# The second MLP matrix over the latents by seven block products for eight, with its operands formed where the first matrix leaves

## The chip, the cores and the metric

The kernel runs on one core of a Trainium2 chip. The metric is the device time of one execution in microseconds (us). The core's engines run side by side and meet only at semaphores: PE (TensorE) multiplies matrices, DVE (VectorE), ACT (ScalarE) and POOL (GpSimd) work element by element, and SP (SyncE) issues the transfers between the chip's memory (HBM) and the core's own memory (SBUF). PE leaves its sums in PSUM, in banks of 128 x 512 numbers. Each engine takes its instructions in the order in which the built program lists them, so one that waits holds back all that stand behind it.

## The reference, cut to what matters

Two layers work on 1024 latent tokens and 256 context tokens of width 1024. In each layer three token mixers (attention, a Fourier mix, a gated long convolution) are put together by an output projection, and a squared-ReLU MLP of hidden width 4096 follows. Each sub-layer is normalised and modulated: the six modulation vectors of a layer (shift, scale and gate of either sub-layer) are products of SiLU(c) with `w_mod`.

```
sh1, sc1, g1, sh2, sc2, g2 = modulation(c, w_mod[l], b_mod[l])      # likewise for c_ctx
hx = modulate(rms_norm(x, norm1_g[l]), sh1, sc1)
px = hx @ w_in[l]
...
x = x + g1 * heads_out(att_x, px, hy, w_out[l])
h = modulate(rms_norm(x, norm2_g[l]), sh2, sc2)
x = x + g2 * (square(relu(h @ w_mlp1[l])) @ w_mlp2[l])
if not last:                       # layer 0 alone does the same for the 256 context tokens
    ...
return rms_norm(x, final_norm_g)
```

The change concerns `square(relu(h @ w_mlp1)) @ w_mlp2`, a product of (1024 x 4096) with (4096 x 1024) in each layer, and the modulation vectors of layer 1.

## The kernel before, in words

Everything is kept transposed: channels lie on the 128 partitions, tokens on the free axis. Every fp32 product is made of three fp32r products (`mm3`, L146 to L150): each operand is split into a high part (ACT casts it) and a low part (the operand less its high part), and hi x hi, hi x lo and lo x hi are added up in one PSUM bank. `wsplit` (L138 to L145) splits a weight tile of 128 x 1024, the low part on POOL (L144); `split_sb` (L156 to L158) splits an activation tile, the low part on DVE or, where it is given `G`, on POOL (L158).

The stages of a layer follow each other: normalisation and input projection, attention with the other mixers beside it, the output projection (two calls of `half_k`, over the two halves of the 1024 inputs), the MLP's first matrix (`up`), its second (`down`), and the next layer's normalisation or the final one.

`up` already uses the Winograd form of Strassen's scheme: weights and activations are cut into 2 x 2 blocks, sums and differences of blocks are formed, and seven block products (`prod`) stand for eight. For each of its 16 steps it forms four 128 x 512 blocks of the hidden activations, takes ReLU (L1254) and the square (L1248) on ACT, and stores them in `d_u` in HBM.

`down` is a plain product. For each of eight slices of 512 hidden channels, `load` fetches four tiles of `d_u` and splits them, with the low parts on POOL; `half_k` then runs over four weight tiles (`mg`), three column chunks of tokens (0 to 512, 512 to 1024, and in layer 0 the context, 1024 to 1280) and two halves, 12 matmuls to a PSUM bank. `resid` (L1127, DVE) takes each bank, multiplies it by the gate and adds it to the residual stream `xT` (latents) or `xC` (context). The last slice is done chunk by chunk in `last_passes`, so that the next normalisation can begin behind the first chunk.

The modulation vectors are made on DVE, one instruction with an accumulated output (L171) for each 128 channels and stream; each reads a weight tile `wm` of 512 KB, for which there are two buffers. For layer 1 all six vectors (64 such instructions over 48 tiles) are made as a side job, `late`, under layer 0's `down`.

The side jobs are Python generators: `spawn(rate, job)` adds one to the background and `tick()`, called after each group of matmuls, takes as many steps of it as the rate says. What the order of the instructions on each engine is in the end, a scheduler decides when the program is built; the rows of the built program show it.

## Time and profile before

| | us |
|---|---|
| median of 3 runs (3231.13 to 3231.99) | 3231.6 |
| the profiled execution's own time | 3233.92 |
| its span, first to last instruction | 3232.2 |
| PE busy in the span | 3028.6 (94%) |
| DVE / POOL / ACT busy | 1884.2 / 1514.3 / 1364.2 |

The stages that the change touches, by the profiled execution's own clock (us from the start of the span):

| stage | layer 0 | layer 1 |
|---|---|---|
| output projections | 769 to 895 | 2407 to 2498 |
| first MLP matrix, `up` | 895 to 1322 | 2498 to 2841 |
| second MLP matrix, `down` | 1322 to 1798 | 2841 to 3220 |

A share of busy time is a mean over unlike stages; a stage's own windows say more. Durations are those of one execution, whose own time lies 2.3 us above the median.

### The profile page before, as it was taken

What the parts mean: (1) busy time and instruction counts of PE and PEld (TensorE: products, weight loads), DVE (VectorE), ACT (ScalarE), POOL (GpSimd) and SP (SyncE); (2) the same over time, 40 slices, a digit from 0 to 9 for tenths busy, and PEclk for the clock granted to TensorE, in tenths of its full rate; (3) what the DMA queues carried; (4) which work ended last, traced back from release to release, by engine and by line L of the source; (5) the groups of instructions that cost most, each with busy time, mean ns of one, the idle gap of its engine ahead of it and who ended that gap; (6) DMA issues with size and microseconds to landing.
All of it is one profiled execution on the core that took longest, in us unless ns stands there. A gap on an engine that the chain in (4) does not pass through costs nothing. (4 is left out here: it accounts for less than half of the span.)

```text
span 3232.2 us, 42677 instructions
## 1 busy us (share of the span) xinstructions
PE 3028.6 (94%) x15756; PEld 2516.0 (78%) x15756; DVE 1884.2 (58%) x2909; ACT 1364.2 (42%) x2425; POOL 1514.3 (47%) x987
## 2 busy tenths in 40 slices
PE   5999998999989999999999999998999799999998
PEld 1787886887768888787888787887887688878886
DVE  7895679886485222297324635779874753322226
ACT  4324475675344444321122423576763444432113
POOL 6434437542555444564442324437535655464333
PEclk8999998999999999999999998999999899999998
DMA  6453563434424322657213233743343343362213
GB/s 241 154 194 114 199 182 89 112 96 165 129 98 141 106 97 90 233 199 259 103 68 104 88 110 102 239 124 89 77 176 111 127 157 105 108 228 92 90 60 111
DMA packets 168280, 433.34 MB, mean 134 GB/s; under 512 B 38086, under 2 KB 55911, under 8 KB 167816
## 3 DMA queue, kind: packets, MB, share of 16 engines
q1 hardware_dynamic: 155064, 388.86, 36.9%
q0 software_dynamic: 9504, 34.67, 3.5%
q10 hardware_dynamic: 3504, 7.08, 0.6%
q8 instruction: 125, 2.05, 0.3%
q14 instruction: 83, 0.68, 0.1%
HBM read 326.21 MB, written 104.33 MB: 133 GB/s over the span
## 5 line engine op out<-in xcount | busy, mean ns | idle before, releaser
L144 POOL TENSOR_TENSOR wl<-wr,wh 128x1024 fp32r<-128x1024 f32 (+2 forms) x274 | 650.0, 2375 | 990.7 <-ACT wh L143 985.5
L143 ACT CAST wh<-wr 128x1024 fp32r<-128x1024 f32 (+2 forms) x274 | 277.8, 1014 | 846.7 <-PE pso L149 385.0
L1127 DVE SCALAR_TENSOR_TENSOR xT<-pso,modc,xT 128x512 f32<-128x512 f32 (+1 forms) x328 | 239.5, 735 | 468.3 <-PE pso L150 436.4
L148 PE MATMUL pso<-uh,wh 128*128 128x512 f32 (+1 forms) x1312 | 488.5, 374 | 13.5 <-DVE xT L1127 5.2
L149 PE MATMUL pso<-ul,wh 128*128 128x512 f32 (+1 forms) x1312 | 484.1, 369 | 6.7 <-POOL ul L158 6.6
L150 PE MATMUL pso<-uh,wl 128*128 128x512 f32 (+1 forms) x1312 | 483.6, 369 | 4.1 <-POOL wl L144 4.1
L1027 POOL TENSOR_SCALAR p<-p,st 128x1280 f32<-128x1280 f32 (+1 forms) x144 | 182.9, 1271 | 263.9 <-DVE st L1022 111.9
L148 PEld LDWEIGHTS pso<-uh,wh 128*128 128x128 f32 x1312 | 250.5, 191 | 59.7 <-DVE xT L1127 7.5
L149 PEld LDWEIGHTS pso<-ul,wh 128*128 128x128 f32 x1312 | 251.2, 191 | 53.4 <-POOL ul L158 10.7
L150 PEld LDWEIGHTS pso<-uh,wl 128*128 128x128 f32 x1312 | 250.3, 191 | 49.3 <-POOL wl L144 5.0
L158 POOL TENSOR_TENSOR ul<-ur,uh 128x512 fp32r<-128x512 f32 (+1 forms) x152 | 197.4, 1328 | 66.3 <-ACT uh L157 61.4
L154 DVE TENSOR_TENSOR pt<-pst,pt 128x512 fp32r<-128x512 f32 x328 | 214.7, 681 | 12.0 <-ACT pt L153 10.6
L153 ACT CAST pt<-pst 128x512 fp32r<-128x512 f32 x328 | 181.9, 590 | 85.1 <-PE pst L1048 66.8
L171 DVE SCALAR_TENSOR_TENSOR junk<-wm,crow 128x1024 bf16<-128x1024 f32 x128 | 193.4, 1533 | 38.3 <-DMA wm<-wmod 37.5
L149 PE MATMUL psi<-hl,wh 128*128 128x512 f32 (+1 forms) x536 | 199.4, 372 | 4.9 <-POOL hl L251 2.5
L148 PE MATMUL psi<-hh,wh 128*128 128x512 f32 (+1 forms) x536 | 201.7, 377 | 1.8 <-ACT hh L254 1.1
L150 PE MATMUL psi<-hh,wl 128*128 128x512 f32 (+1 forms) x536 | 198.2, 370 | 3.0 <-POOL wl L144 3.0
L1066 PE MATMUL pv<-pt,v 128*128 128x256 f32 x656 | 172.1, 297 | 15.2 <-DVE pt L154 13.9
L1302 DVE TENSOR_TENSOR wr<-wr 128x512 f32<-128x512 f32 x32 | 37.5, 1173 | 247.7 <-POOL wl L144 242.4
L1067 PE MATMUL pv<-pt,v 128*128 128x256 f32 x656 | 168.0, 292 | 6.0 <-DVE pt L154 5.8
L1048 PE MATMUL pst<-ident,p 128*128 128x128 f32 x1024 | 147.6, 278 | 23.1 <-DVE pt L154 10.9
L1014 DVE TENSOR_REDUCE st<-sx 128x1 f32<-128x1024 f32 x128 | 155.7, 1216 | 14.9 <-PE sx L150 14.3
(413 smaller groups left out, 7580.0 us busy)
## 6 DMA issues: line engine op xcount, KB each, us to landing
wr<-w SPq DMA_DIRECT2D x158, 512.0 KB, 3.6
wm<-wmod SPq DMA_DIRECT2D x80, 512.0 KB, 3.6
d_u<-c SPq DMA_DIRECT2D x128, 256.0 KB, 3.0
ur<-d_u SPq DMA_DIRECT2D x30, 640.0 KB, 5.6
tb<-ftab POOLq DMA_DIRECT2D x34, 512.0 KB, 4.7
ur<-d_u SPq DMA_DIRECT2D x30, 512.0 KB, 4.1
wr<-wout SPq DMA_DIRECT2D x28, 512.0 KB, 4.0
wr<-win SPq DMA_DIRECT2D x26, 512.0 KB, 3.2
```

The costliest lines, as they stand in the source:

```text
L143: S.copy(hi[:, n0:n], t[:, n0:n])
L144: G.tensor_tensor(lo[:, n0:n], t[:, n0:n], hi[:, n0:n].bitcast(F32), op=ALU.subtract)
L148: T.matmul(ps, lhsT=lh, rhs=rh, start=first, stop=False)
L149: T.matmul(ps, lhsT=lh, rhs=rl, start=False, stop=False)
L150: T.matmul(ps, lhsT=ll, rhs=rh, start=False, stop=last)
L153: S.copy(hi, ps)
L154: V.tensor_tensor(lo, ps, hi.bitcast(F32), op=ALU.subtract)
L158: (eng or V).tensor_tensor(lo, src, hi.bitcast(F32), op=ALU.subtract)
L171: V.scalar_tensor_tensor(jk, w, 1.0, crow[:, st, :], op0=ALU.mult, op1=ALU.mult, accum_out=modc[:, l, st, n : n + 1])
L1027: G.tensor_scalar(pr, pr, st[:, 5:6], 1.0, op0=ALU.mult, op1=ALU.mult)
L1066: T.matmul(pv[:, :256], lhsT=vt[:, kt, :], rhs=th, start=j == 0, stop=False)
L1127: V.scalar_tensor_tensor(x, ps[:, : c1 - c0], g, x, op0=ALU.mult, op1=ALU.add)
```

## The change

**Seven products.** In `down`, the first seven of eight parts of the hidden axis (512 channels each, two blocks of 128 pairs: `g` is 0 to 6) are multiplied by the same Winograd form as in `up`. A step (`g`, `j`) takes a weight tile, cut into four blocks of 128 x 256, and makes seven products of six matmuls each (two 128-deep blocks, three fp32r products), where the plain form needs eight. `direct` splits the weight blocks that are used as they are, `combined` forms the four weight combinations on DVE and splits them. Three of the seven products go to the residual at once through `resid`; the other four belong to more than one output block and are added up over all `g` in sums on the core (`sums`; one of them lies in the unused half of `xT`), which `combine` puts together at the end (16 gated additions to `xT` and 16 additions among sums in each layer). The eighth part (`g` 7) is done as before, by `half_k`. The context, in layer 0, keeps its plain product (`context`).

**Operands.** The activations come in seven forms: b11, b21, b22 as they are and t1 to t4, differences of blocks. `up` forms t1 and t3 on DVE and t2 and t4 on POOL for its first 14 steps (`operands`, L1272 to L1281 of the new file), in tiles that it had at hand, and stores seven tiles of 128 x 512 for each step in `d_t` in place of four in `d_u`. `down` fetches and splits them (`fetch`): low parts of t3 and t4, in layer 0 also of t2 and of the context's tiles, on DVE; the others on POOL.

**Modulation.** Layer 1's six vectors are no longer made under layer 0's `down`. Those of its first sub-layer (40 instructions, 24 tiles) are made under layer 0's output projections, those of its second (24 instructions, 24 tiles) under layer 1's.

**Smaller edits.** `last_passes` puts the sums together ahead of the last products of each chunk, and the context's normalisation for layer 1 is begun after the others. The two tiles of `d_u` that `up` loaded early for `down` are gone.

```diff
+            def operands(j, b11, b12, b21, b22):
+                t1, t2, t4 = spare
+                V.tensor_tensor(t1, b12, b11, op=ALU.subtract)
+                G.tensor_tensor(t2, b22, t1, op=ALU.subtract)
+                V.tensor_tensor(b12, b22, b12, op=ALU.subtract)
+                G.tensor_tensor(t4, b21, t2, op=ALU.subtract)
+                for name, t in (("t1", t1), ("t3", b12), ("t2", t2), ("t4", t4)):
+                    nc.sync.dma_start(out=d_t[j, name], in_=t)
...
+            pairs = {name: 4 if not ctx and name in ("b11", "t1", "t2") else 3 for name in SEVEN}
+            sums = {n: [ps_.tile([128, 512], F32, name=f"s{n}{j}") for j in range(4)] for n in (1, 6, 7)}
+            sums[5] = [xT[2 * j + 1][0][:, 512:] for j in range(4)]
...
+            def fetch(src, n, pool, tag, bufs, eng):
+                hi, lo = (pool.tile([128, n], F32R, tag=tag, bufs=bufs, name=tag) for _ in range(2))
+                nc.sync.dma_start(out=lo.bitcast(F32), in_=src)
+                split_sb(hi, lo, lo.bitcast(F32), eng)
+                return hi, lo
...
+            def direct(w):
+                a22 = w[:, 768:1024]
+                hi, lo = wsplit(w, 1024 if ctx else 512)
+                if not ctx:
+                    S.copy(hi[:, 768:], a22)
+                    G.tensor_tensor(lo[:, 768:], a22, hi[:, 768:].bitcast(F32), op=ALU.subtract)
+                return hi, lo
+
+            def combined(w):
+                a11, a12, a21, a22 = (w[:, 256 * i : 256 * i + 256] for i in range(4))
+                r = [nt("r") for _ in range(2)]
+                V.tensor_tensor(r[0][:, :256], a21, a22, op=ALU.add)
+                V.tensor_tensor(r[0][:, 256:], r[0][:, :256], a11, op=ALU.subtract)
+                V.tensor_tensor(r[1][:, :256], a12, r[0][:, 256:], op=ALU.subtract)
+                V.tensor_tensor(r[1][:, 256:], a11, a21, op=ALU.subtract)
+                hi, lo = wsplit(r[0], 512)
+                S.copy(hi[:, 512:], r[1])
+                G.tensor_tensor(lo[:, 512:], r[1], hi[:, 512:].bitcast(F32), op=ALU.subtract)
+                return hi, lo
+
+            def product(g, j, n, w, c, name):
+                ps = psp.tile([128, 512], F32, tag="ps", name="psw")
+                for q in range(2):
+                    ks = slice(c + q * 128, c + q * 128 + 128)
+                    mm3(ps, w[0][:, ks], w[1][:, ks], *at[g, name, q], q == 0, q == 1)
+                if n in sums:
+                    t = sums[n][j]
+                    if g == 0:
+                        S.copy(t, ps)
+                    else:
+                        V.tensor_tensor(t, t, ps, op=ALU.add)
+                else:
+                    u, t = {2: (0, 0), 3: (0, 512), 4: (1, 0)}[n]
+                    resid(l, 5, 2 * j + u, t, t + 512, ps, xT)
...
+                later = spawn(2 if last else 1.2, modulation(1, crow, (4, 3, 5) if last else (1, 0, 2), lambda s: (0, 1) if s < 2 else (0,),
+                                                             mod_load))
                 half_k(l, 2, a["wout"][l, 1], cat, chs, xT, psp, raw[4])
-                finish()
+                settle(jobs)
...
             for (c0, c1), ac, g in todo:
+                if c0 == 512:
+                    settle(later)
```

In the built program the matmuls of 128 x 512 on the MLPs' second matrix fall from 2976 to 2640 over both layers; those of 128 x 256, the context's and the last half chunk's, stay at 960.

Three places show how the order moves. Line numbers shift: L1127 becomes L1136 (`resid`), L144 L153 (`wsplit`), L158 L167 (`split_sb`), L171 L180 (modulation).

The first is DVE in layer 0's output projections, in the second group of weight columns, before (`pso` is a finished bank, `cat` a split tile of the mixers' outputs):

```order
L1127 SCALAR_TENSOR_TENSOR xC_7426<-pso,modc,xC_7426 128x256
L158 TENSOR_TENSOR cat_10241_7960<-wr,cat_10240_7959 128x256
L1127 SCALAR_TENSOR_TENSOR xC_7428<-pso,modc,xC_7428 128x256
L1127 SCALAR_TENSOR_TENSOR xT_7429<-pso,modc,xT_7429 128x512
L1127 SCALAR_TENSOR_TENSOR xT_7431<-pso,modc,xT_7431 128x512
L1127 SCALAR_TENSOR_TENSOR xT_7429<-pso,modc,xT_7429 128x512
L1127 SCALAR_TENSOR_TENSOR xT_7431<-pso,modc,xT_7431 128x512
```

The same place in the change, where `junk,modc<-wm,crow` is a modulation instruction:

```order
L180 SCALAR_TENSOR_TENSOR junk,modc<-wm,crow 128x1024
L1136 SCALAR_TENSOR_TENSOR xT_7529<-pso,modc,xT_7529 128x512
L180 SCALAR_TENSOR_TENSOR junk,modc<-wm,crow 128x1024
L1136 SCALAR_TENSOR_TENSOR xC_7528<-pso,modc,xC_7528 128x256
L1136 SCALAR_TENSOR_TENSOR xC_7530<-pso,modc,xC_7530 128x256
L167 TENSOR_TENSOR cat_01_8054<-wr,cat_00_8053 128x512
L167 TENSOR_TENSOR cat_5121_8056<-wr,cat_5120_8055 128x512
L167 TENSOR_TENSOR cat_10241_8058<-wr,cat_10240_8057 128x256
L180 SCALAR_TENSOR_TENSOR junk,modc<-wm,crow 128x1024 x4
L1136 SCALAR_TENSOR_TENSOR xT_7531<-pso,modc,xT_7531 128x512
```

Modulation instructions, one to four at a time, now stand between the instructions that empty PE's banks.

The second place is layer 1's `down`, away from its ends. DVE before did nothing there but empty banks:

```order
L1127 SCALAR_TENSOR_TENSOR xT_25597<-pso,modc,xT_25597 128x512
L1127 SCALAR_TENSOR_TENSOR xT_25598<-pso,modc,xT_25598 128x512
L1127 SCALAR_TENSOR_TENSOR xT_25591<-pso,modc,xT_25591 128x512
L1127 SCALAR_TENSOR_TENSOR xT_25592<-pso,modc,xT_25592 128x512
L1127 SCALAR_TENSOR_TENSOR xT_25591<-pso,modc,xT_25591 128x512
```

DVE in the change, about one step (`psw` is a finished bank, `s` a sum, `r` a combination of weight blocks, `t_...` an operand's low part):

```order
L1136 SCALAR_TENSOR_TENSOR xT_26559<-psw,modc,xT_26559 128x512
L1421 TENSOR_TENSOR xT_26559<-xT_26559,psw 128x512
L1402 TENSOR_TENSOR r<-wr 128x256
L1405 TENSOR_TENSOR r<-wr 128x256
L167 TENSOR_TENSOR t_28736<-t_28736,t_28735 128x512
L1421 TENSOR_TENSOR s_26582<-s_26582,psw 128x512
L1403 TENSOR_TENSOR r<-r,wr 128x256
L1136 SCALAR_TENSOR_TENSOR xT_26558<-psw,modc,xT_26558 128x512
L1404 TENSOR_TENSOR r<-wr,r 128x256
L1421 TENSOR_TENSOR s_26586<-s_26586,psw 128x512
L1421 TENSOR_TENSOR s_26579<-s_26579,psw 128x512
```

DVE now has seven banks to empty in a step, four weight combinations and a low part or two among them.

The third place is SP's queue where layer 0's `down` begins. Before, the first splits' sources came behind the last stores of `up` but for two (`ur` is a tile of `d_u`):

```order
L1249 DMA d_u_134<-c 128x256
L134 DMA wr<-w 128x1024 x2
L1339 DMA ur<-d_u_103 128x256
L1339 DMA ur<-d_u_104 128x256
L1339 DMA ur<-d_u_105 128x1280
L134 DMA wr<-w 128x1024
L1339 DMA ur<-d_u_106 128x1280
L1249 DMA d_u_134<-c 128x512 x2
```

In the change:

```order
L1365 DMA t_12787<-d_t0t_137 128x512
L1365 DMA t_12792<-d_t0t_140 128x512
L1365 DMA t_12807<-d_t0t_141 128x512
L1258 DMA d_u_134<-c 128x256
L1365 DMA t_12822<-d_t1t_144 128x512
L1365 DMA t_12827<-d_t1t_147 128x512
L1365 DMA t_12842<-d_t1t_148 128x512
L1365 DMA t_12993<-d_t2t_151 128x512
L1365 DMA t_13106<-d_t2t_154 128x512
L143 DMA wr<-w 128x1024
L1365 DMA t_13153<-d_t2t_155 128x512
L1365 DMA b_12797<-d_t0b_135 128x512
```

The operands t2, t3 and t4 of the first products, whose tiles lie where `up` needs nothing any more, are now fetched ahead of all others.

## Rows read from the trace of the kernel before

**Rows 1.** The page: busy time by engine; the chain that ended last.
```profile
PE 3028.6 (94%) x15756; PEld 2516.0 (78%) x15756; DVE 1884.2 (58%) x2909; ACT 1364.2 (42%) x2425; POOL 1514.3 (47%) x987
...
PE 23%; DVE 4%; POOL 1%; ACT 1%; issue 1%; DMA 1%; ACTq 0%; POOLq 0%; DVEq 0%
```

**Rows 2.** Windows of the stages: length, busy time by engine, granted clock, DMA share, GB/s.
```profile
1322.00:1798.00 476.00, 459.07 (x2322) 385.81 (x2322) 267.32 (x364) 112.79 (x171) 223.57 (x136) 0.99 0.46 164
...
2498.00:2841.00 343.00, 323.37 (x1355) 258.41 (x1354) 168.17 (x199) 152.29 (x231) 187.00 (x96) 0.97 0.38 122
2841.00:3220.00 379.00, 366.72 (x1652) 301.18 (x1652) 132.15 (x176) 93.37 (x135) 174.59 (x103) 0.98 0.34 115
```

**Rows 3.** Windows: a stretch of layer 1's second matrix, 128x512 matmuls alone.
```profile
2950.00:3180.00 230.00, 230.00 (x998) 187.18 (x997) 68.17 (x88) 47.45 (x61) 94.27 (x55) 1.00 0.23 76
```

**Rows 4.** Timeline, PE: context matmuls, the 1st and 25th (start, us, instruction).
```profile
782.13 0.28 PE L148 MATMUL pso<-cat,wh 128*128 128x256 f32 x1
...
784.95 0.40 PE L148 MATMUL pso<-cat,wh 128*128 128x512 f32 x1
```

**Rows 5.** Windows: layer 0's second matrix while the modulation runs beside it.
```profile
1380.00:1540.00 160.00, 150.94 (x761) 126.56 (x760) 136.80 (x191) 27.89 (x43) 86.28 (x46) 0.98 0.68 242
1430.00:1480.00 50.00, 46.47 (x226) 39.47 (x226) 43.54 (x57) 9.47 (x15) 30.27 (x16) 0.93 0.61 210
```

**Rows 6.** Groups, 1380 to 1540: count | busy us, mean ns | idle before, who ended it.
```profile
L148 PE MATMUL pso<-uh,wh 128*128 128x512 f32 x166 | 66.9, 403 | 4.9 <-DVE xC L1127 3.8 <-DVE xT L1127 1.1
...
L158 POOL TENSOR_TENSOR ul<-ur,uh 128x512 fp32r<-128x512 f32 x23 | 43.4, 1914 | 31.0 <-ACT uh L157 31.0
...
L148 PE MATMUL pso<-uh,wh 128*128 128x256 f32 x88 | 25.8, 293 | 4.1 <-DVE xT L1127 4.0
```

**Rows 7.** Groups of the page: the modulation instruction, its whole count.
```profile
L171 DVE SCALAR_TENSOR_TENSOR junk<-wm,crow 128x1024 bf16<-128x1024 f32 x128 | 193.4, 1533 | 38.3 <-DMA wm<-wmod 37.5
```

**Rows 8.** Windows: output projections up to the first latent chunk's end, either layer.
```profile
769.00:870.00 101.00, 98.53 (x510) 82.94 (x510) 53.76 (x84) 36.64 (x63) 41.74 (x25) 0.98 0.41 126
...
2407.00:2476.00 69.00, 68.25 (x296) 55.53 (x297) 27.97 (x42) 21.91 (x33) 25.23 (x14) 1.00 0.33 105
```

**Rows 9.** Timeline, DVE near the end (start, us, instruction, idle before it).
```profile
3191.09 0.42 DVE L211 TENSOR_TENSOR facc<-facc,sq 128x256 f32<-128x256 f32 x1 [0.55 <-ACT sq L209]
...
3192.40 2.34 DVE L211 TENSOR_TENSOR facc<-facc,sq 128x256 f32<-128x256 f32 x1 [0.49 <-ACT sq L209]
```

**Rows 10.** Timeline, POOL at the same place.
```profile
3192.08 2.38 POOL L144 TENSOR_TENSOR wl<-wr,wh 128x1024 fp32r<-128x1024 f32 x1 [2.21 <-ACT wh L143]
```

**Rows 11.** Groups, 1560 to 1770, layer 0's second matrix without the modulation.
```profile
L1127 DVE SCALAR_TENSOR_TENSOR xT<-pso,modc,xT 128x512 f32<-128x512 f32 x62 | 46.5, 750 | 109.5 <-PE pso L150 109.5
L144 POOL TENSOR_TENSOR wl<-wr,wh 128x1024 fp32r<-128x1024 f32 x19 | 45.7, 2403 | 120.0 <-ACT wh L143 120.0
...
L158 POOL TENSOR_TENSOR ul<-ur,uh 128x512 fp32r<-128x512 f32 x22 | 28.1, 1296 | 5.7 <-ACT uh L157 5.7
...
L1127 DVE SCALAR_TENSOR_TENSOR xC<-pso,modc,xC 128x256 f32<-128x256 f32 x26 | 12.6, 484 | 20.7 <-PE pso L150 20.7
...
L158 POOL TENSOR_TENSOR ul<-ur,uh 128x256 fp32r<-128x256 f32 x12 | 8.6, 739 | 3.6 <-PE pso L150 3.6
```

**Rows 12.** Groups, DVE, 769 to 832: splits with both sources in SBUF.
```profile
L158 DVE TENSOR_TENSOR cat<-raw,cat 128x512 fp32r<-128x512 f32 x8 | 5.2, 687 | 0.2 <-ACT cat L157 0.2
L158 DVE TENSOR_TENSOR cat<-raw,cat 128x256 fp32r<-128x256 f32 x4 | 1.7, 421 | 0.0
```

**Rows 13.** Groups, DVE, 2600 to 2800, first matrix: SBUF sources; a PSUM source.
```profile
L1303 DVE TENSOR_TENSOR wr<-wr 128x512 f32<-128x512 f32 x12 | 12.6, 1046 | 0.1
...
L1316 DVE TENSOR_TENSOR s<-s,psm 128x512 f32<-128x512 f32 x12 | 8.2, 686 | 27.4 <-PE psm L150 27.4
```

**Rows 14.** Windows: the first 18 and 25 us of the second matrix.
```profile
1322.00:1340.00 18.00, 13.93 (x50) 9.23 (x50) 3.86 (x6) 9.18 (x20) 14.85 (x14) 0.91 0.78 277
2841.00:2866.00 25.00, 18.58 (x70) 13.86 (x70) 6.48 (x10) 12.61 (x22) 19.12 (x14) 0.86 0.69 254
```

More of the change, by code (lines that the diff above doesn't have):

```diff
@@ new lines, in down @@
+            todo = [(g, j) for g in range(7) for j in range(4)]
+            raw = lambda g, j: wload(a["w2"][l, g, j], 1024)
+            parts_of["at"] = 2
+            w = raw(0, 0)
+            C, D = combined(w), direct(w)
+            drain(load(0))
+            load_back()
+            column = {1: (0, "b11"), 2: (256, "b21"), 4: (768, "t4"), 5: (0, "t1"), 6: (256, "t2"), 3: (512, "b22"), 7: (768, "t3")}
+            for n, (g, j) in enumerate(todo):
+                if j == 0:
+                    ahead = spawn(1, load(g + 1))
+                w = raw(*todo[n + 1]) if n + 1 < len(todo) else None
+                order = [6, 7, 1, 5, 4, 2, "D", 3] if n == 0 else [1, 2, 4, "D", 5, 6, 3, 7]
+                if ctx:
+                    order[6:6] = ["c0", "c1", "C"]
+                    if j:
+                        order.remove("D")
+                        order.remove("c0"), order.remove("c1"), order.remove("C")
+                        order[3:3] = ["c0", "c1", "D", "C"]
+                else:
+                    order.insert(order.index("D") + 1, "C")
+                later = C, D
+                for i, what in enumerate(order):
+                    if what == "D":
+                        later = later[0], direct(w) if w is not None else None
+                    elif what == "C":
+                        later = combined(w) if w is not None else None, later[1]
+                    elif what in ("c0", "c1"):
+                        context(g, j, D, int(what[1]))
+                    else:
+                        if j == 3 and what == 5:
+                            settle(ahead)
+                        product(g, j, what, D if what in (1, 2, 4) else C, *column[what])
+                    if i % 3 == 2:
+                        tick()
+                C, D = later
```

285 lines of the change are left out of this document (165 added, 120 removed).

## The prediction

> **What bounds the kernel now.** I read the page first, then windows over the stages, then groups and timelines inside the stages that change. On the page PE is busy for 94% of the span, and the chain that ended last goes mostly through PE [rows 1]: the kernel as a whole is bound by its matmuls. By stages it is the same: layer 0's second matrix takes 476 us with PE busy for 459, layer 1's takes 379 with 367 [rows 2]. A busy PE is a pipelined one, so what a matmul costs is read from its pace. In a stretch of layer 1 without a gap, 998 matmuls of 128x512 take 230.0 us, 0.2305 us each at a granted clock of 1.00, the upper of the two levels (2.4 GHz) [rows 3]; 24 of the context's 128x256 take 784.95 - 782.13 = 2.82 us, 0.1175 each [rows 4]. DVE and POOL have room before: in layer 1's second matrix 132 and 175 us of 379 [rows 2]. The question is what is left of that room when PE has an eighth less to do and they have more.
>
> **The change part by part**, against the profiled execution's own 3233.9 us.
>
> *Matmuls taken away.* The instruction lists give 2976 - 2640 = 336 fewer matmuls of 128x512, 168 a layer: 336 x 0.2305 = **-77.4 us**, all on the path as long as PE is what the stage waits for.
>
> *Modulation out of layer 0's second matrix.* Between 1380 and 1540 DVE is busy for 137 of 160 us, and PE's idle time before new banks, 4.9 + 4.1 us, is ended by DVE's `resid` [rows 5, 6]. In 1430 to 1480 the granted clock is 0.93: 0.07 x 50 = 3.5 us more [rows 5]. With the side job gone I count all of it: **-12.5 us** (from 0, if the new work puts DVE in the same state, a cost that I count below).
>
> *Modulation under the output projections.* One instruction is 1.53 us [rows 7], with the read of its accumulator 1.61. Layer 0 gets 40: 64.5 us. Until its first latent chunk ends, from which the next normalisation starts, DVE has 101 - 53.8 = 47.2 us free [rows 8]; 17 us are left over. In the built order they stand in front of the instructions that empty PE's banks, and the wait is for the chunk's last bank, so DVE's delay passes on to the normalisation and to the first matrix. I take **+17** (0, if PE's eight banks of head start swallow it, to 64, if no idle time can be used). Layer 1 gets 24, 38.7 us, into 69 - 28 = 41 us free [rows 8]; it fits, but the first must wait for its vector to be loaded: **+4** (0 to 39).
>
> *What DVE and POOL do to each other.* Two low parts that read only SBUF show it. A 128x256 addition takes 0.42 us at 3191.09, while POOL is idle, and 2.34 us from 3192.40 to 3194.74; POOL's weight split runs from 3192.08 to 3194.46 [rows 9, 10]. DVE waited for POOL's whole instruction and then did its own 0.3 us later. In the other direction POOL's 128x512 split takes 1.30 us without the modulation beside it and 1.91 with it [rows 6, 11]. Instructions of DVE whose one source is PSUM do not show it: `resid` is 0.75 us [rows 11], an addition from a bank 0.69 [rows 13]. The Trainium skill ("SBUF — State Buffer", Who interferes with whom) states it as a rule: a DVE instruction with two SBUF inputs and a GpSimd one that reads SBUF exclude each other for a whole instruction; the trace agrees, with 2.34 us for 0.42. By that rule POOL's time and DVE's two-source time in a step add up and may not exceed the step, which speaks against this change in layer 1, where it would charge 16 us; without the rule that charge would be nothing.
>
> *A step of layer 1* (one of 28): PE 42 x 0.2305 = 9.68 us. POOL, at the prices of rows 11: two halves of `combined` at 1.30, `direct` 1.30 + 0.74, and 10 operand splits in 4 steps, 2.5 x 1.30: 7.87 us. DVE from PSUM: 3 x 0.75 + 4 x 0.69 = 4.99; from SBUF: four combinations of 256 at 0.42 and one split at 0.69 [rows 12], 2.37. POOL and DVE's SBUF work together are 10.24 us, above PE's 9.68. DVE's waits: in the first matrix its 128x512 combination is 1.05 us instead of 0.69, 0.36 longer [rows 12, 13], with POOL busy for 187 of 343 us, 55% [rows 2]. At 7.87 / 9.68 = 81% that is 0.53, so DVE has 7.36 + 5 x 0.53 = 10.0. I take 10.4 us for a step, a little above both, since queues that are full never line up: 0.72 x 28 = **+20** (0, if the waits fall into gaps, to 117, if each of the five waits for a whole split of 1.30: 13.9 us a step).
>
> *A step of layer 0*: PE 9.68 + 24 x 0.1175 = 12.50 us. POOL 2 x 1.30 + 2.40 + 2 x 1.30 = 7.6; DVE 5.96 from PSUM (two context banks of 0.48 with it) and 3.13 from SBUF, with waits of 0.36 x 0.61 / 0.55 = 0.40 on 6.5 instructions 11.7. Both stay under PE: **+5** for disorder (0 to 27, the 8% that PE lost in rows 5, over 28 steps).
>
> *Putting the sums together.* 32 DVE instructions a layer at about 0.72 us, 23 us, most of them in the last four steps, where layer 1's DVE then has 27 + 23 = 50 us for PE's 39. PE can be eight banks ahead, 8 x 1.38 = 11 us. **+8** for both layers (0 to 20).
>
> *First matrix.* Two more DVE and two more POOL instructions in each of 14 steps a layer, and three more stores. PE hides them: in layer 1 POOL is busy for 55% and DVE for 49% of the stage [rows 2]; in the built order the next weight splits stand ahead of the two that wait for the squares. If that cover failed, 2.6 us of POOL in 28 steps would come out, 73; I take **+2**, as the row on POOL's share is the nearest.
>
> *Start of the second matrix.* PE idles for 4.1 and 6.4 us there and loses 0.09 x 18 and 0.14 x 25 us to the clock, 15 in all [rows 14]. t2, t3 and t4 are now fetched while the first matrix ends, so the first twelve matmuls find their operands; the next ones wait for tiles that come free with the last matmul. **-4** (-15 to +10).
>
> *Transfers.* A step of layer 1 moves 14 tiles of 256 KB over four steps and one of 512 KB, about 148 GB/s where 277 were reached [rows 14]: nothing.
>
> Sum: -77.4 - 12.5 + 17 + 4 + 20 + 5 + 8 + 2 - 4 = **-37.9 us**. The profiled execution lies 2.3 us above the median of 3231.6; on the median this gives 3193.7, say **3194 us**.
>
> **Rivals.** *PE stays the only bound.* The waits of DVE and POOL fall into PE's lead, and nothing is charged for steps and sums: -37.9 - 33 = -70.9, **3161 us**. For it: the first matrix runs a Winograd step with PE busy throughout and DVE's waits hidden. Against it: there POOL was at 55%, here it would be at 81%, and both together above 100%.
>
> *DVE and POOL become the bound in layer 1.* The mechanism is the exclusion shown above, the place layer 1's 28 steps, with layer 0's at 8%: the price 117 - 20 and 27 - 5 more, -37.9 + 119 = +81, **3313 us**. It decides from the point where a step of layer 1 takes 10.4 + 37.9 / 28 = 11.75 us, which is a mean wait of 0.9 us at each of DVE's five SBUF instructions; below that the kernel is still faster. For it: four of the five stand close together, so that each can find the next split of POOL before it, and at 3192.40 the wait was whole. Against it: a DVE that falls behind also feeds POOL later, which then stands less in its way.
>
> *The modulation costs more where it went than it did where it was.* The clock halves in the longer gap before the first matrix, and layer 1's does not fit: 17 + 4 becomes about 45, and the sum -14, **3218 us**. Against it: 24 us of that have no row behind them.
>
> **How the numbers follow.** The forecast has 0.52 (its own range 3172 to 3213), PE alone 0.25, the modulation 0.12, DVE and POOL as the bound 0.11. Leaving out half of the last and the far end of the second, the range is 3150 to 3236. Within 0.2%, 6.5 us, which is about what a measurement of this kernel can tell from no change, I put 0.06, from between the modulation's case and the bound's; faster 0.82, slower 0.12.
>
> **What would show it.** Right: 128x512 matmuls of the second matrix at 0.23 us in the mean of a step in layer 0, and idle time before them in layer 1 that is ended by DVE's additions from banks or POOL's splits, some 20 us; DVE's 256-wide combinations at 0.8 to 1.0 us instead of 0.42; a first matrix of layer 0 that starts 15 us later against the start of the output projections. Wrong: layer 1's second matrix without such gaps and some 310 to 340 us long (PE alone), or longer than its 379 us of before (the bound).

## The result, and the profile after

The changed kernel takes 3285.9 us (median of 4 runs, 3278.97 to 3292.92) against 3231.56: **1.0168 times as long, interval 1.0144 to 1.0192**. Forecast were 3194 us and a range of 3150 to 3236; the sign is wrong. The profiled execution took 3292.92 us, 59.0 more than the one of before; it lies 7.0 us above its median, the one of before 2.3.

The page after, busy time and the chain that ended last, against [rows 1]:

```profile
PE 3002.3 (91%) x15420; PEld 2476.8 (75%) x15420; DVE 2344.2 (71%) x3491; ACT 1480.5 (45%) x2682; POOL 1763.0 (54%) x1165
...
PE 10%; POOL 3%; issue 3%; DVE 2%; DMA 1%; ACT 1%; SPq 0%; POOLq 0%; DVEq 0%; ACTq 0%
```

PE issued the 336 matmuls less, but is busy for only 26 us less in a span that is 59 us longer. The windows of the stages, in order of time, beside [rows 2]: layer 0's output projections and second matrix, layer 1's output projections, first and second matrix (columns as in [rows 2]: length, then busy us of PE, weight loads, DVE, ACT and POOL; clock, DMA share, GB/s).

```profile
776.00:922.00 146.00, 125.21 (x592) 103.11 (x593) 129.36 (x187) 50.55 (x81) 70.38 (x34) 0.91 0.61 204
1353.00:1818.00 465.00, 428.73 (x2152) 360.15 (x2151) 377.04 (x494) 163.14 (x272) 263.98 (x158) 0.96 0.39 132
2432.00:2539.00 107.00, 96.13 (x393) 76.56 (x392) 83.55 (x109) 35.37 (x50) 47.99 (x23) 0.92 0.70 240
2539.00:2892.00 353.00, 326.98 (x1356) 259.11 (x1355) 190.37 (x236) 153.54 (x236) 233.89 (x128) 0.96 0.46 156
2892.00:3279.00 387.00, 346.81 (x1482) 274.10 (x1482) 319.09 (x409) 149.32 (x272) 273.12 (x198) 0.94 0.41 142
```

Layer 1's second matrix was to lose 38.7 us of matmuls and takes 387 us where it took 379. In both second matrices DVE is now busy for more than 80% (it was 56% and 35%), and the granted clock is below 0.97. What PE waited for in the seven-product steps, first layer 0 (1353 to 1748), then layer 1 (2892 to 3211); columns: waited for, us in total, times, longest. `t` and `b` are operands' tiles, `uc` the context's, `wh` and `wl` the weights' high and low parts:

```profile
PE psw L158 <- DVE t L167: 18.7, 6, 5.5
...
PE psw L158 <- POOL b L167: 8.5, 5, 2.9
PE psw L157 <- ACT t L166: 3.8, 1, 3.8
PE psw L159 <- POOL wl L153: 3.3, 1, 3.3
```

In layer 0 there are six waits for an operand's low part in seven groups of four steps: one at each change of group, 8 to 12 us into the new group. In layer 1 the waits end in more places, most often at a low part that POOL itself made. Windows of layer 0 inside a group (four steps' time) and over the next change:

```profile
1430.00:1480.00 50.00, 50.00 (x261) 42.83 (x261) 39.19 (x56) 17.28 (x29) 26.26 (x17) 0.98 0.35 116
1480.00:1535.00 55.00, 52.01 (x261) 44.43 (x260) 44.57 (x62) 16.27 (x27) 31.01 (x21) 0.94 0.33 113
```

Both hold 261 matmuls. Inside a group PE runs without a gap, 12.5 us a step as computed; with a change the same work takes 5 us more, 3 of waiting and about 2 of clock (0.98 - 0.94 = 0.04 of 55 us). The change itself, in three timelines (start, us, instruction, in brackets the idle time before it). PE:

```profile
1480.08 0.40 PE L157 MATMUL psw<-t,wh 128*128 128x512 f32 x1
1483.47 0.79 PE L158 MATMUL psw<-t,wh 128*128 128x512 f32 x1 [2.99 <-DVE t L167]
```

DVE, which makes that low part at 1482.33:

```profile
1473.11 1.52 DVE L1402 TENSOR_TENSOR r<-wr 128x256 f32<-128x256 f32 x1
1474.55 1.52 DVE L1405 TENSOR_TENSOR r<-wr 128x256 f32<-128x256 f32 x1
...
1477.43 1.78 DVE L167 TENSOR_TENSOR t<-t,t 128x512 fp32r<-128x512 f32 x1
1479.14 2.60 DVE L167 TENSOR_TENSOR uc<-uc 128x256 fp32r<-128x256 f32 x1
1481.66 0.74 DVE L1136 SCALAR_TENSOR_TENSOR xT<-psw,modc,xT 128x512 f32<-128x512 f32 x1
1482.33 1.09 DVE L167 TENSOR_TENSOR t<-t,t 128x512 fp32r<-128x512 f32 x1
```

POOL beside it:

```profile
1474.31 2.92 POOL L167 TENSOR_TENSOR b<-b,b 128x512 fp32r<-128x512 f32 x2
1477.19 1.49 POOL L167 TENSOR_TENSOR t<-t,t 128x512 fp32r<-128x512 f32 x1
1478.62 2.83 POOL L153 TENSOR_TENSOR wl<-wr,wh 128x1024 fp32r<-128x1024 f32 x1
1481.42 1.45 POOL L167 TENSOR_TENSOR b<-b,b 128x512 fp32r<-128x512 f32 x1
```

POOL has one split behind the other and no pause. DVE's 256-wide instructions take 1.52, 1.52 and 2.60 us where 0.42 is their own time [rows 12], and the last of them ends 0.3 us after POOL's weight split. Each held the other up: that split takes 2.83 us where 2.40 is its own time [rows 11]. `resid`, which reads a PSUM bank, keeps its 0.74. Over these instructions DVE loses (1.52 - 0.42) x 2 + 1.78 - 0.69 + 2.60 - 0.42 + 1.09 - 0.69 = 5.9 us; PE waits 3.0.

The 59.0 us by stage, from first to last matmul in the two profiled executions. "Main" is the stretch from the first matrix's end to the last passes; in layer 0 its loss is what remains after the matmuls and the modulation are taken off. A group is priced at PE's pace, 4 x 12.50 = 50.0 us in layer 0 and 4 x 9.68 = 38.7 in layer 1:

| | forecast, us | measured, us |
|---|---|---|
| matmuls taken away | -77.4 | -77.4 |
| modulation out of layer 0's second matrix | -12.5 | -14.9 (by the run with the move alone) |
| output projections, layer 0 / layer 1 | +17 / +4 | +20.0 / +16.9 |
| first matrix, layer 0 / layer 1 | +2 in all | +3.0 / +9.4 |
| main of the second matrix, layer 0 / layer 1 | +5 +20 -4 = +21 in all | +38 / +38 = +76 |
| of it, groups 1 to 6, layer 0 / layer 1 | +5 / +20 (all groups) | +31 / +25 |
| of it, group 0 with the stage's start, layer 0 / layer 1 | -4 in all | +6 / +13 |
| last passes, layer 0 / layer 1 | +8 in all | +5.4 / +8.8 |
| stretches that the change doesn't touch, tail | 0 | +7.4 + 3.7 + 0.3 |

Nothing in the change explains the last row; the two executions' distances from their medians differ by 4.7 us.

### The profile page after: what moved, and what is told of

Read it like the earlier page. It is cut to its first block, busy times and chain, and to the rows that moved or that the text cites. A ratio compares the mean times of both kernels' runs of the same rounds, so it can differ in the third digit from the quotient of the medians.

```text
span 3291.1 us, 43722 instructions
## 1 busy us (share of the span) xinstructions
PE 3002.3 (91%) x15420; PEld 2476.8 (75%) x15420; DVE 2344.2 (71%) x3491; ACT 1480.5 (45%) x2682; POOL 1763.0 (54%) x1165
## 5 line engine op out<-in xcount | busy, mean ns | idle before, releaser
L153 POOL TENSOR_TENSOR wl<-wr,wh 128x1024 fp32r<-128x1024 f32 (+2 forms) x274 | 631.2, 2308 | 609.1 <-ACT wh L152 598.0
L152 ACT CAST wh<-wr 128x1024 fp32r<-128x1024 f32 (+2 forms) x274 | 264.8, 968 | 586.4 <-PE psm L158 275.3
L180 DVE SCALAR_TENSOR_TENSOR junk<-wm,crow 128x1024 bf16<-128x1024 f32 x128 | 189.6, 1504 | 35.3 <-DMA wm<-wmod 33.9
L158 PE MATMUL psi<-hl,wh 128*128 128x512 f32 (+1 forms) x536 | 201.1, 375 | 3.8 <-POOL hl L260 2.3
L158 PE MATMUL psw<-t,wh 128*128 128x512 f32 x448 | 181.4, 405 | 23.1 <-DVE t L167 21.5
L157 PE MATMUL psw<-t,wh 128*128 128x512 f32 x448 | 180.4, 403 | 9.9 <-ACT t L166 7.9
L159 PE MATMUL psw<-t,wl 128*128 128x512 f32 x448 | 179.0, 400 | 0.0
L1023 DVE TENSOR_REDUCE st<-sx 128x1 f32<-128x1024 f32 x128 | 155.5, 1214 | 16.0 <-PE sx L159 15.5
L167 POOL TENSOR_TENSOR b<-b,b 128x512 fp32r<-128x512 f32 x96 | 134.7, 1413 | 53.8 <-ACT b L166 48.6
L1029 ACT ACTIVATE p<-sx,st,acol 128x1024 f32<-128x1024 f32 x128 | 153.8, 1201 | 0.0
L1075 PEld LDWEIGHTS pv<-pt,v 128*128 128x128 f32 x656 | 129.5, 197 | 27.5 <-DVE pt L163 20.7
L1136 DVE SCALAR_TENSOR_TENSOR xT<-psw,modc,xT 128x512 f32<-128x512 f32 x168 | 122.6, 741 | 36.3 <-PE psw L159 36.2
L1057 PEld LDWEIGHTS pst<-ident,p 128*128 128x128 f32 x1024 | 118.3, 144 | 37.8 <-issue 16.5
```

What stands on the lines that cost most here:

```text
L152: S.copy(hi[:, n0:n], t[:, n0:n])
L153: G.tensor_tensor(lo[:, n0:n], t[:, n0:n], hi[:, n0:n].bitcast(F32), op=ALU.subtract)
L157: T.matmul(ps, lhsT=lh, rhs=rh, start=first, stop=False)
L158: T.matmul(ps, lhsT=lh, rhs=rl, start=False, stop=False)
L159: T.matmul(ps, lhsT=ll, rhs=rh, start=False, stop=last)
L180: V.scalar_tensor_tensor(jk, w, 1.0, crow[:, st % crow.shape[1], :], op0=ALU.mult, op1=ALU.mult, accum_out=modc[:, l, st, n : n + 1])
```

## The experiments

Theories: **A, handover**: operands come late since their tiles come free late. **B, load**, later sharpened to **D, exclusion**: POOL's splits hold DVE up at the group changes. **C**: the moved modulation. Ratios are to the kernel before, measured anew beside each run (medians 3232 to 3237 us), with 95% intervals; the changed kernel has 1.0168. "Us less" is the difference of two ratios, times 3231.6. Stages are read from each run's profiled execution. The edits are cut to what matters.

**Operands that stay.**
```
-  at[g, name, q] = fetch(...)
+  t = fetch(..., tag of its own); at[g, name, q] = t if g == 0 else at[0, name, q]
```


> The changed kernel, but in the second matrix every product reads the operands of group 0, which stay where they are; those of groups 1 to 7 are fetched and split at the same places as before into a pair of tiles of their own that no matmul reads. So all the work of DMA, ACT, DVE and POOL stays, and no matmul waits for a handed-over operand (the sums over groups 1 to 7 are of the wrong operands). Theory A (handover: at each of the six group changes a layer the next group's operands come late, 55 us a group instead of 50 in layer 0, 43.2 instead of 38.7 in layer 1): 6 x 5 + 6 x 4.5 = 57 us go, 3229 us. Theory B (load: DVE and POOL have too much to do in a step whatever waits for it): the load is the same, 3286 us within 8. Theory C (the moved modulation is what was lost): 3286 too.

1.0295 [1.0272, 1.0319], 3327 us: slower than either theory said. Nothing held the fetches back any more, and the scheduler put the splits of all groups into the first four. Windows of layer 0, with these splits and behind them:

```profile
1420.00:1590.00 170.00, 135.17 (x619) 104.36 (x618) 143.27 (x172) 78.34 (x140) 120.81 (x78) 0.95 0.53 170
1590.00:1740.00 150.00, 149.58 (x788) 127.72 (x789) 106.41 (x165) 26.37 (x36) 59.44 (x36) 1.00 0.14 46
```

So the run doesn't keep the load in its place and can't part A from B. It shows that a loss of this size needs no handover (PE waited there for banks that DVE had not emptied, 15.0 and 13.6 us between 1400 and 1600), and that without operand splits the same steps run at PE's pace.

**Thin splits, both engines; POOL's alone; DVE's alone.**
```
   S.copy(hi, raw)
-  eng.tensor_tensor(lo, raw, hi, op=subtract)
+  eng.tensor_tensor(lo[:, :p], raw[:, :p], hi[:, :p], op=subtract)   # p = 64 from group 1 on
```


> The changed kernel, but the low parts of the second matrix's operands of groups 1 to 7 are formed for 64 of 512 columns only (the other columns keep the unsplit value): order, waits and transfers stay, and about 1.1 us of POOL or 0.6 of DVE goes from each of the 56 (layer 1) or 60 and more (layer 0) operand splits after the first group. Theory A as pure latency (tile free, transfer, copy, split in a row take longer than the 8 us between an operand's last use and its next first use): group changes stay as they are, 3286 - 10. Theory A as a burst in the queues (the refill's splits stand in one row on POOL and DVE): the 57 us of the group changes go for the most part, 3225 to 3245. Theory B (load in all steps): 57 us and more go, 3229 or less, and gaps inside steps go as well as those at the group changes.

> The changed kernel with thin operand splits (64 of 512 columns, other columns unsplit) for POOL's operands alone (b11, b21, b22, t1; in layer 1 t2 too); DVE's stay whole. With both engines' thin, 72 us went. Exclusion (DVE's instructions on SBUF wait for POOL's whole instructions, so that POOL's row at a group's change makes DVE late): 50 to 70 of the 72 go, 3215 to 3236 us, and layer 0's gaps, which DVE's t ends, go too. POOL's own work alone: only layer 1's gaps, which POOL's b ends, go, 3250. DVE's own work: 3270.

> The changed kernel with thin operand splits for DVE's operands alone (t3, t4, in layer 0 t2 and the context's); POOL's stay whole. Exclusion: a thin instruction of DVE still waits for POOL's whole one, and only its own 0.6 us goes: 10 to 25 us, 3261 to 3276. DVE's own work as the cause: layer 0's gaps go, 36 us or more, 3250 or less.

Both 0.9944 [0.9929, 0.9958], 72 us less than the changed kernel; POOL's alone 0.9948 [0.9936, 0.9960], 71 less; DVE's alone 1.0097 [1.0080, 1.0115], 23 less. The fetches and the handover of tiles are the same in all three, so A falls: the time of POOL's splits is the cause. The length of a group, from its first matmul to the next group's, us:

| | layer 0: group 0 | groups 1 to 6 | layer 1: group 0 | groups 1 to 6 |
|---|---|---|---|---|
| the changed kernel | 63.8 | 52.9 to 57.3 | 58.0 | 41.2 to 43.9 |
| both thin | 62.3 | 50.1 to 50.2 | 50.7 | 38.9 to 39.0 |
| POOL's thin | 64.9 | 50.1 to 50.5 | 52.6 | 38.9 to 39.0 |
| DVE's thin | 64.1 | 51.9 to 55.7 | 56.2 | 40.4 to 43.5 |
| all on DVE (below) | 62.4 | 50.7 to 53.4 | 50.0 | 38.9 to 41.8 |

With POOL's thin, both layers run at PE's pace from group 1 on, and layer 0's low part from DVE, left whole, is in time (group of PE in that run, 1354 to 1721; the last number is PE's idle time before these matmuls):

```profile
L158 PE MATMUL psw<-t,wh 128*128 128x512 f32 x224 | 89.1, 399 | 0.0
```

With DVE's own thin it is still late, in layer 0 (waits, 1353 to 1743):

```profile
PE psw L158 <- DVE t L1368: 16.4, 6, 3.8
```

though it is nearly no work any more. DVE, then POOL, at a group change of that run:

```profile
1475.47 1.32 DVE L1368 TENSOR_TENSOR t<-t,t 128x64 fp32r<-128x64 f32 x1
...
1485.87 0.21 DVE L1368 TENSOR_TENSOR t<-t,t 128x64 fp32r<-128x64 f32 x1
```
```profile
1475.22 1.49 POOL L1368 TENSOR_TENSOR t<-t,t 128x512 fp32r<-128x512 f32 x1
```

The same 64 columns take 1.32 us beside POOL's split, ending 0.1 us after it, and 0.21 us when POOL has none. That is D, for layer 0.

In layer 1 it is not shown alone. There the waits end at POOL's own parts, as behind the change at 3039 (PE, then POOL):

```profile
3049.82 0.80 PE L158 MATMUL psw<-b,wh 128*128 128x512 f32 x1 [2.74 <-POOL b L167]
```
```profile
3038.39 3.03 POOL L167 TENSOR_TENSOR b<-b,b 128x512 fp32r<-128x512 f32 x2 [1.24 <-ACT b L166]
3041.38 3.02 POOL L167 TENSOR_TENSOR t<-t,t 128x512 fp32r<-128x512 f32 x2
3044.35 1.83 POOL L153 TENSOR_TENSOR wl<-wr,wh 128x512 fp32r<-128x512 f32 x1
3046.15 1.18 POOL L1396 TENSOR_TENSOR wl<-wr,wh 128x256 fp32r<-128x256 f32 x1
3047.29 2.48 POOL L167 TENSOR_TENSOR b<-b,b 128x512 fp32r<-128x512 f32 x2
```

Eight splits without a pause take 11.4 us; the prices of [rows 11] give 7 x 1.30 + 0.74 = 9.8. DVE's instructions thus added some 1.5 us to a row that is long by itself, and no run parts the two shares of the 2.7 us that PE waits here.

**The next group's fetch a step later; two sets of tiles in layer 1.**
```
-  if j == 0: ahead = spawn(1, load(g + 1))
+  if j == 1: ahead = spawn(1, load(g + 1))
```


> The changed kernel, but the side job that fetches and splits the next group's first operands begins with a group's second step instead of its first; nothing is left out. Theory A as a burst (in the first step of a group the urgent second operands of this group and the not yet urgent first ones of the next stand mixed in one row, 16 us of POOL in 15): more than half of the 57 us at the group changes goes, and some of the 20 us at the two starts, 3235 to 3260 us. Theory B: the same load in a group, no gain, 3286 within 8. Theory C: 3286.

```
-  pairs: 4 for b11, t1, t2 in layer 1, else 3
+  pairs: 4 for all but b22 in layer 1 (no third weight set)
```


> The changed kernel, complete, with four pairs of tiles instead of three for b21, t3 and t4 in layer 1's second matrix (six of the seven operands then have two whole sets; the third set of weight parts and the sixth weight tile make room), so that their second operands can be fetched a group ahead. Theory A (handover): layer 1's 27 us at the group changes shrink to less than 10, 3262 us. Theory D (the load itself, bunched or not): 3280 or more, as the room for weights is less too.

1.0189 [1.0168, 1.0210] and 1.0152 [1.0139, 1.0165]. The later fetch changes nothing: PE's waits for DVE's t are 18.5 us in 6 again, and a group's transfers stand in one row on SP's queue in nearly the same order as before, so the edit did not part the urgent ones from the others. In the other run the tiles are free a group ahead, and layer 1's second matrix is only 5 us shorter: the late part is now that of the weights, which POOL splits in the same row (waits, 2897 to 3206). That the run has one set of weight parts and one weight tile less has a share in it, which it doesn't show:

```profile
PE psw L159 <- POOL wl L153: 16.7, 10, 3.2
```

**The splits moved to DVE.**
```
-  fetch(..., V if name in ("t3", "t4") or ctx and name == "t2" else G)
+  fetch(..., V)                                          # all; also the last group's
+  fetch(..., V if ctx or name[0] == "t" else G)          # the other run: some
```


> The changed kernel, complete, with every operand split of the second matrix's groups on DVE (0.69 us each, where POOL took 1.30): POOL keeps the weights alone, as in the run with POOL's splits thin (3219 us). Exclusion as the cause: what DVE pays in its own time (8 x 0.69 = 5.5 us of 50 a group in layer 0, 10 x 0.69 = 6.9 of 38.7 in layer 1) is less than the waits that go; layer 0 comes back to 50 us a group (-30), layer 1, whose DVE is then at 9.1 us of 9.68 in a step before any wait, gains 0 to 15: 3240 to 3256 us. POOL's split time as such or the number of splits on any engine as the cause: no gain or a loss, 3286 or more.

> As the run with all operand splits on DVE, but in layer 1 POOL keeps b11, b21 and b22 (6 of 14 in a group): both engines' time on SBUF then adds up to 9.3 us of a step's 9.68 there. Exclusion: layer 0 -30, layer 1 -10 to -20, 3236 to 3246 us, and the better of the two. Otherwise 3286 or more.

All: 1.0004 [0.9991, 1.0017], 53 us less than the changed kernel and level with before. Some: 1.0062 [1.0046, 1.0078]. The busier engine got 64 and 78 splits more to do in the two layers, and the kernel is faster for it, by more than the expectation gave (3240 to 3256 us; the median is 3235.9). Layer 0 and layer 1, second matrix, all on DVE, in an execution of 3250.6 us, 15 above that median:

```profile
1360.00:1803.00 443.00, 423.06 (x2154) 353.06 (x2152) 389.40 (x560) 164.11 (x274) 178.26 (x94) 0.98 0.41 139
2877.00:3236.00 359.00, 333.98 (x1478) 270.00 (x1479) 338.16 (x485) 149.05 (x272) 174.47 (x120) 0.96 0.45 152
```

POOL is busy for 178 and 174 us instead of 264 and 273; DVE for only 12 and 19 more, though 64 and 78 splits of 0.69 us are 44 and 54 us of work: the rest is waits that went. That layer 1 would want some on POOL was wrong: DVE at 94% (359 us) does better than both engines sharing (377).

**The splits moved to the first matrix, in a row or spread over the next step.**
```
+  for name, t in (the seven operands):            # in up
+      split_sb(hi, t, t, G if name in ("t2", "t4") else V); store hi and t
```


> The changed kernel, complete, but the seven operands of groups 0 to 6 are split where they are formed, in the first matrix (98 copies by ACT and 98 subtractions by DVE and POOL in each layer, 24 us of work in each of 14 steps spread over three engines), and both parts are stored and fetched; the second matrix fetches two tiles where it fetched one and splits nothing but weights, the context's tiles and the last group. Theory D (the operand splits, bunched at a group's change on POOL and DVE that shut each other out, are what ate the matmuls): the gain of the thin splits, about 70 us, stays but for up to 10 in the first matrix: 3215 to 3230 us. Rival E (the work costs wherever it stands): the first matrix grows by what the second gives back, 3270 to 3290. Rival F (twice the fetches, about 240 GB/s in layer 1, become the bound): layer 1's second matrix stays above 375 us, 3250 or more.

> As the run that split the operands where they are formed (3397 us; its first matrices took 94 and 88 us longer than before, its second matrices ran at PE's pace), but a step's operands are formed and split in the middle of the next step, one after another between the weight splits, instead of in one row at the step's end. If the row at the end was what cost (the next step's first weights stood behind it on ACT and POOL): the first matrices come back to within 15 us of before each, 3225 to 3250 us. If DVE, POOL and ACT have no room for this work in the first matrix (rival E): 3370 or more.

1.0497 [1.0477, 1.0518] and 1.0380 [1.0367, 1.0394], 3397 and 3359 us. Of the rivals only E points this way, but the loss is some three times what it allowed (3270 to 3290). Windows of the first run, layer 0's first and second matrix:

```profile
922.00:1443.00 521.00, 443.89 (x2118) 363.07 (x2119) 358.78 (x307) 232.46 (x396) 313.41 (x156) 0.92 0.46 164
1444.00:1880.00 436.00, 418.34 (x2148) 350.94 (x2147) 314.38 (x458) 115.72 (x181) 175.01 (x101) 0.99 0.57 201
```

The second matrix gains 29 us (24 in layer 1), the first pays 91 (78), though DVE is busy for only 69% and POOL for 60% there: PE waited for weights' parts behind the splits (POOL's wl 24.2 us, 1100 to 1443). Spread over the next step, PE waits for DVE's banks instead (20.7 us), and the first matrix still takes 497. Transfers (rival F) are not the bound: layer 1's second matrix took 362.

**The move alone; no modulation; modulation spread; both.**
```
   # on the kernel before: late modulation out of down, under the output projections
   # on the changed kernel: no loads and products for layer 1
   # on the changed kernel: 24 (layer 0) and 8 (layer 1) products in up
```


> The kernel before with one part of the change alone: layer 1's modulation stands under the two layers' output projections instead of under layer 0's second matrix; the second matrix stays as it was. By the forecast's prices: 17 + 4 - 12.5 = +8.5 us against before, 3241 us. By the stages of the changed kernel (output projections +20 and +17, layer 1's first matrix +9): 46 - 12.5 = +33, 3265 us. If layer 1's first matrix was slowed by the new second matrix's stores and not by the modulation: +24, 3256 us.

> The changed kernel without the loads and products of layer 1's modulation (its shifts, scales and gates then come from the biases alone), which stood under both layers' output projections. Theory C (the move is what was lost: output projections 20 and 17 us longer than before, layer 1's first matrix 9): 46 us go, 3240 us. By the price of the forecast for it (17 + 4 = 21): 3265 us. Theories A and B leave the second matrix as it is: two stages of 466 and 383 us.

> The changed kernel, complete, with the modulation's products spread: 16 instead of 40 under layer 0's output projections and 24 in its first matrix, 16 instead of 24 under layer 1's and 8 in its first matrix. If the output projections lose what does not fit into DVE's free time (47 and 41 us, rows of the stage), 26 us of work fit and both stages return to within 5 us of before: -30, 3256 us. If the weights that they load through the first matrix's own ring delay it, this is given back there: 3280 or more.

> The changed kernel, complete, with the operands split in the first matrix and the modulation spread over output projections and first matrices. Theory D with the modulation's own price: the two gains add, 3286 - 65 - 30 = 3190 us, below both kernels. Rival E: the first matrices, which now take both, become bound by DVE, and the sum is lost: 3250 or more.

1.0048 [1.0029, 1.0067], +15.5 us; 1.0053 [1.0038, 1.0067], 37 less than the changed kernel; 1.0239 [1.0216, 1.0262]; 1.0379 [1.0358, 1.0400]. The first two lie between the times that their theories gave, 3253 and 3252 us; the last two came out as their slower rivals had it. In the first, layer 0's projections take 144 us for 126, layer 1's 99 for 91, and layer 0's second matrix 461 for 476. Without modulation the projections are back at 125 and 91, but layer 1's first matrix stays at 354, and with the move alone it is at 343 as before: its 9 us come with the operands that are formed and stored there. Spread, layer 0's projections take 127 us, but its first matrix 460 for 430: work put there comes out of PE's time as the splits did (these weight tiles also went through the first matrix's own buffers, and the run doesn't part that from DVE's time). In after, layer 1's projections take 107 us and not 99 as with the move alone. Most of these 8 us is one wait that the move alone doesn't have, at 2493 (waits of after, 2432 to 2539):

```profile
PE pso L157 <- ACT wh L152: 5.6, 1, 5.6
```

ACT's cast of the weights stood there behind a square that waited for DVE. What made DVE later than in the move alone is not shown.

**The rest: gate vector later, ends, order of ACT's queue** (all on the kernel with the splits on DVE, the first on that with some).
```
+  modulation(1, crow, (5,), ...) in layer 1's up, tiles of its own
+  w0 = wsplit(raw(7, 0)) in the last step; t2, t3 fetched ahead of the first weights
+  (the same, and) settle(later) behind the second chunk, rate 0.9
+  half_k: next weights split ahead of the squares, squares a step later, third weight set
```


> As the run with some of layer 1's splits on DVE, and with the 8 products of layer 1's last modulation vector (the MLP's gate) in its first matrix, with weight tiles of their own, instead of under its output projection. If the projection loses what does not fit (24 products of 1.61 us in 41 us free): 5 to 9 us less than that run. If the first matrix gives them back (as when its weight ring was shared): no difference or slower.

> As the run with all operand splits on DVE (3236 us, equal to before), complete, with two waits of PE taken away in each layer's second matrix: the last group's first weights are loaded and split inside the last product step (PE waits 3.1 + 2.2 and 3.5 + 2.2 us for them now, and the clock is at 0.5 for 6.8 us behind each), and the first product's operands are fetched ahead of the first weights (5.4 us at layer 1's start, 0.5 for 10.2 us behind it). If these gaps are what stands in the way: 9 + 9 + 5 us at most, 3213 to 3226 us, below both kernels. If the next wait stands right behind (the norm's rows, the operands of the next products): 3230 or more.

> As the run just named (ends of the second matrix), with layer 0's modulation at rate 0.9 instead of 1.2 and finished only behind the second latent chunk of the output projection, not ahead of it. If the projection's 18 us are DVE's delay of the first chunk's normalisation: 5 to 12 us less than that run, 3205 to 3220. If the modulation then delays the second chunk's normalisation or the first matrix's squares: no less.

> As the run with all operand splits on DVE (equal to before), complete, with the output projections and the last passes ordered so that ACT casts a step's weights without standing behind squares that wait for DVE: the next weights are cast ahead of the squares, the squares come one step later, and the projections have a third set of weight parts. If the lost time there is ACT's queue (the cast waits behind a square that waits for a DVE held up by the modulation or the sums: 4.9 + 3.8 + 2.8 + 2.9 us of idle PE in layer 0's projection with the clock at 0.5 for 20 us, 4.8 + 2.1 in layer 1's, 3.1 + 1.9 and 3.5 + 2.0 in the last passes): half or more of some 40 us, 3205 to 3220 us. If the later squares delay the normalisations as much: 3230 or more.

1.0073 [1.0057, 1.0088]; 1.0007 [0.9994, 1.0020]; 1.0010 [1.0001, 1.0019]; 1.0011 [0.9996, 1.0025]: none gains. With the gate vector later, layer 1's projection takes 97 us for 105 and its first matrix 360 for 350. With layer 0's modulation slower, the projection takes 138 for 143 and the first matrix 442 for 430. The gap in the last passes stayed (2.7 us for ACT's wh): it belongs to a later weight tile than the one moved. The last run asked why the projections lose. What PE waited for in layer 0's, in after (776 to 922) and then in that run (777 to 924):

```profile
PE pso L159 <- POOL wl L153: 8.8, 6, 2.9
PE pso L157 <- ACT wh L152: 8.3, 2, 6.0
```
```profile
PE psn L234 <- POOL nacc L220: 14.7, 2, 8.1
PE pso L157 <- DVE xT L1136: 3.0, 1, 3.0
```

The weights' casts were late behind squares that wait for DVE; put ahead of them, the wait moves to POOL's sums of the squares (`nacc`), which now come a step later. So this order gave nothing back; whether another could is not shown. No version that does the whole work beats the kernel before; those with thin splits leave a part of it out.

## Why the prediction was wrong

*The step that failed is the pair of terms for the steps, "+20" for layer 1 and "+5" for layer 0, and with them the start's "-4".* The three were to cost 21 us and cost 76, which is 55 of the 97 us between forecast and measurement. The forecast knew the exclusion and had its rows [rows 9, 10], but spread its price evenly: a mean wait of 0.36 to 0.53 us at each of DVE's instructions on SBUF, "Both stay under PE". Away from a change this is right, PE loses nothing. But the fetches of a group's second operands, and the next group's first, come free together with the last products of a group; their splits stand in one row on POOL, and there DVE waits at every instruction on SBUF, up to 2.2 us. Five us a change in layer 0 and four in layer 1, six changes each, are the +31 and +25 of the table; thin POOL splits gave back 57 us between the first matrices and the last passes, 71 in the whole kernel. Layer 0, with "7.6" and "11.7" us in a step of 12.50, was to be safe and lost the most. Layer 1's +20 came near its 25, but by luck: the forecast spread it over all steps as DVE's waits, and it was lost behind the changes, mostly at parts that POOL made late.

*Start, -4*: +20, 6 in layer 0 and 13 in layer 1. Group 0 takes 62.3 and 50.7 us even with both engines' later splits thin, for 50.0 and 38.7 of matmuls; only what that gives back (63.8 to 62.3, 58.0 to 50.7) belongs to those splits. The changed kernel's first 25 us of layer 1's second matrix, against [rows 14]:

```profile
2892.00:2917.00 25.00, 18.55 (x50) 11.63 (x51) 8.40 (x11) 14.36 (x27) 15.17 (x13) 0.73 0.93 324
```

50 matmuls instead of 70 and a clock of 0.73 instead of 0.86, while the transfers run at 324 GB/s and 93% of the DMA engines. That "the first twelve matmuls find their operands" is right in layer 0, where they run without a gap, but PE then waits six times up to 1378, 0.6 to 4.1 us each; in layer 1 PE waits 3.8 us before the very first. The run with the changed ends fetched two operands ahead of the first weights, and layer 1's main stretch stayed at 292 us; so the cause of the longer start is not shown.

*First matrix, +2*: 12. *Layer 1's output projection, +4*: 17, of which 9 come with the move alone. *Right*: the matmuls' price, -12.5 for the modulation (14.9), +17 under layer 0's projection (20), and within 6 us the sums (+8; 14). DVE's 256-wide combinations of layer 1 have means of 0.77 to 1.13 us, about as foretold (0.8 to 1.0): the mean was right, and said little on where the waits lie.

The rival that named the mechanism had the right sign, but not the place: its point of decision, 11.75 us for a mean step of layer 1, was not reached (315 / 28 = 11.3). Its sign, a second matrix of layer 1 longer than 379 us, did come (387), with the start and the last passes in it. The sum turned because many terms were low at once: the steps 31 us (layer 0, priced at 27 at most, lost 31 in groups 1 to 6 alone), the start 24, the projections 16, the first matrices 10, the sums 6. The rule of the Trainium skill ("SBUF — State Buffer", Who interferes with whom), that a DVE instruction with two SBUF inputs and a GpSimd one that reads SBUF exclude each other for a whole instruction, is borne out by the 1.32 us for 64 columns. That "POOL's time and DVE's two-source time in a step add up" had to be asked of the ten us or so behind a change, where POOL has no pause, not of a mean step.

What stays open: with all splits on DVE, the second matrices are 18 and 19 us shorter than in the run with the move alone, and yet the kernel is only level with before. Against the 37 us stand 15 of the move, 6 and 9 in the first matrices, and 8 in layer 1's projection (these from the execution of 3250.6 us; layer 0's first matrix differs by 7 us between executions of kernels that do the same there). Open are also the shares of POOL's own row and of the exclusion in layer 1, and the cause of the longer starts.

## What to carry to other kernels

Price two engines that hold each other up over the shortest stretch in which their work stands in a row, not over the mean step: ask which tiles come free together and what queues up then. Work moved to a busier engine can be a gain, if the engine that loses it held the other one up; a thin instruction (64 of 512 columns, with all its waits) shows which engine's time it is. A stage with PE at 94 to 96% and the other engines at 39 to 55%, as the first matrices of before, has not half of their time to give away: 98 splits put there cost 0.8 to 0.9 us each.

## What the hardware showed

A DVE subtraction of 128x64 took 0.21 us alone and 1.32 us beside POOL's 128x512 split of 1.49. The waits of PE of 3 us in layer 0's full stream were each followed by a stretch at a granted clock of 0.5 (1.2 GHz), and the 55 us around one of them show 5 us lost. And 64 and 78 splits of 128x512, moved from POOL (1.3 to 1.5 us each) to DVE, raised DVE's busy time by only 12 and 19 us.
